# Transposes of the activated columns in groups of eight, in float32r, from tiles filled by a DMA

## Chip, cores and metric

The kernel runs on one core of one Trainium2 chip. The metric is the device time of one execution in microseconds (us). The short names of the engines are those of the profile: PE is TensorE (matmul), PEld its weight load, DVE is VectorE, ACT is ScalarE, POOL is GpSimd and SP is SyncE, which here only issues DMAs.

## The reference, cut to what matters

One decoder layer over 256 tokens of width 2048, float32 throughout. An input projection, two kinds of attention and an output projection come first; then the part with the change, a feed-forward block of width 8192:

```python
x = x + _rmsnorm(mixed @ w_out[layer], norm_attn_post[layer])

h = _rmsnorm(x, norm_mlp_pre[layer])
u = jnp.square(jax.nn.relu(h @ w_up[layer]))        # 256 x 8192
x = x + _rmsnorm(u @ w_down[layer], norm_mlp_post[layer])
```

## The kernel before, in words

**Split operands.** Every large matmul is done on float32r operands. A float32 value is split into `hi`, which ACT writes rounded to float32r, and `lo`, the remainder, which DVE writes; a product is then three matmuls, hi by hi, lo by hi and hi by lo (`three`, `mm`). Weights come in tiles of 128 x 1024 by DMAs that SP issues, into five `raw` buffers, and are split into eight pairs of `hi` and `lo` buffers, six tiles ahead of their use (`Weights`, `W_AHEAD`).

**The up phase.** The 8192 columns of `w_up` are taken in eight column groups of 1024 (`for j in range(FF // CW)`). Of each group four accumulators of 128 tokens x 512 columns are built in four banks of PSUM, for token block b = 0, 1 and column half n = 0, 1. The first group takes sixteen plain steps over the rows of the weights. Each later group takes five plain steps (`k`, 12 matmuls each) and then three steps of seven products (`w`), with single plain steps between; the seven products need four further banks for the partial sums `m`, and these are the four banks of the previous group (`free`). At the end `close` combines the partial sums into four SBUF tiles `c0` to `c3`.

**The evacuation, `up_evac`.** Each accumulator is evacuated by a chain of its own: DVE adds its `c` tile to it (not in the first group), ACT takes the Relu with the row's scale into a float32 tile `r` (two buffers), PE transposes `r` in four pieces of 128 x 128 into the same bank, now called `rt`, and ACT squares that into `uT`, where the columns lie on partitions as the down projection needs them. The transposes go through `transpose`, which takes the float32 identity `ident` and the float32 data.

**The down phase.** For g = 0 to 15, `split_u(g)` splits `uT[g]` and `down_mm` multiplies it with `w_down`. The evacuation of the last column group runs beside its first matmuls; the banks of that group are taken over for outputs at step (0, 1).

**What sets the order.** The kernel fixes the order of every engine's instructions itself, with a model clock (`Flow`). Each matmul that is written out moves the clock on (`MM`, 0.216 us for 512 columns), each transpose by `TR` = 0.109. Chains such as `up_evac` are generators: `yield t` means that the chain goes on when the clock has moved on by t. `flow.pump()`, called after every three matmuls of the up phase and after every twelve of the down phase, lets the chains that are due write their next instructions. `flow.finish(*chains)` runs chains to their end at once, whatever their delays. The delays place an instruction in the lists; they do not make the chip wait. On the chip each engine works through its own list in order and waits by semaphores.

Of the kernel before, what the change touches and what calls it, by code (L numbers as in the profile page):

```python
# [18 lines left out]
F32 = mybir.dt.float32  # L19
F32R = mybir.dt.float32r  # L20
I32 = mybir.dt.int32
BF16 = mybir.dt.bfloat16
AF = mybir.ActivationFunctionType
OP = mybir.AluOpType
PSUM = bass.MemoryType.PSUM

P = 128
D = 2048
S = 256
NB = S // P  # L30
# [15 lines left out]
CW = 1024  # L46
# [44 lines left out]
D_X0, D_X, D_SS, D_TAB = 6.0, 1.0, 3.0, (16.0, 20.0)  # L91
D_NORM, D_HT, D_SECOND = 4.5, 1.5, 4.0

D_UP, UP_STEP = 1.8, 2.2


N_SEVEN, SUMS_AHEAD = 3, 2
# [6 lines left out]
TR = 0.109  # L104
# [121 lines left out]
def layer(nc, tc, io):  # L226
    flow = Flow()

    def pool(name, side, **kw):
        return tc.alloc_tile_pool(name=name, bufs=1, side=side, **kw)  # L230

    con = pool("con", "left")
# [7 lines left out]
    def bank(i, name):  # L240
        return ps.tile([P, 512], F32, tag=f"bank{i}", bufs=1, name=name)
# [5 lines left out]
    def acc_bank(name):  # L247
        return next_bank(0, 4, name)
# [12 lines left out]
    def transpose(out, a):  # L261
        nc.tensor.transpose(out, a, ident)  # L262
        flow.spend(TR)
# [37 lines left out]
    def up_weight(j, k):  # L301
        return io["w_up"][k * P:(k + 1) * P, j * CW:(j + 1) * CW]

    late = {}
# [29 lines left out]
    for j in range(FF // CW):  # L334
        wide_u.append([])
        for what, k in [("k", k) for k in range(KD)] if j == 0 else UP_STEPS:
            if what == "k":
                ts = [weights.plan(up_weight(j, k), 1, CW, gcol[:, 8 + k:9 + k])]
            else:
                sums, fs = seven(j, k)  # L340
                weights.first[max(len(weights.specs) - SUMS_AHEAD, after)] = sums
                ts = [weights.plan(f) for f in fs]
# [66 lines left out]
    nc.gpsimd.memset(neg_half, -0.5)  # L409
    ident = con.tile([P, P], F32, name="ident")  # L410
    make_identity(nc, ident)
    warm = con.tile([P, 1], F32, name="warm")
    nc.scalar.activation(warm, neg_half, AF.Copy)
    if N_WARM:
# [15 lines left out]
    k = 0  # L430
# [136 lines left out]
    for half in range(2):  # L567
        qkv = {}
        for nm in "qkv":
            accs = [acc for _, _, acc in proj(xT, [ch_a[half, nm]], f"{nm}{half}")]  # L570
            t = pa.tile([P, NB, 512], F32, tag=nm, name=f"{nm}_{half}")
# [135 lines left out]
    rstd2 = [None] * NB  # L707
# [79 lines left out]
    for ns in ((0, 1), (2,), (3,)):  # L787
        if len(ns) == 2:
            order = [(c, t, b) for ts in (range(6), range(6, 8)) for c in range(2) for t in ts for b in range(NB)]
        else:  # L790
            order = [(0, t, b) for t, b in in_order(8, (0, APART[0] if ns == (3,) else 0))]
        for c, b, acc in proj(mixT, [ch_o[n] for n in ns], f"o{ns[0]}", order, heads_done):
            n = ns[c]
            if not late:
# [8 lines left out]
                                  in_=io["norm_attn_post"].partition_broadcast(P).rearrange("p o d -> p (o d)"))  # L803
# [10 lines left out]

    uT, dpl = {}, {}

    def up_evac(j, b, i, acc, order, more=None):

        yield UP_STEP * order
        if more is not None:  # L820
            nc.vector.tensor_tensor(out=acc, in0=acc, in1=more, op=OP.add)  # L821
            yield 1.6
        r = late["up"].tile([P, 512], F32, tag="r", bufs=2, name=f"r{j}_{b}")
        nc.scalar.activation(r, acc, AF.Relu, scale=rstd2[b])  # L824
        yield D_UP if j > 1 else 2 * D_UP
        t = bank(i, f"rt{j}_{b}")
        for k in range(4):
            transpose(t[:, k * P:(k + 1) * P], r[:, k * P:(k + 1) * P])
        if j not in uT:
            tag = {"tag": "WT"[j // 2 - 6], "bufs": 2} if j >= 12 else {}  # L830
            uT[j] = late["up"].tile([P, CW], F32, name=f"uT{j}", **tag).rearrange("p (k s) -> p k s", k=4)
        nc.scalar.activation(uT[j][:, :, b * P:(b + 1) * P], t.rearrange("p (k s) -> p k s", k=4), AF.Square)

    def split_u(g):
        if g == 0:
# [33 lines left out]
    def all_sums():  # L869
        for kp in range(N_SEVEN - 1):  # L870
            yield from left_sums(kp)
        yield 8.0
        yield from left_sums(N_SEVEN - 1)
# [14 lines left out]
        return dict(zip(PARTS, c))  # L888

    PARTS = ((0, 0), (0, 1), (1, 0), (1, 1))  # L890
    evac = []
    for j in range(FF // CW):
        at = {bn: 4 * (j % 2) + i for i, bn in enumerate(PARTS)}
        if j == 0:
            accs = {bn: acc_bank(f"acc_u0_{bn[0]}{bn[1]}") for bn in at}
            at = {bn: (turn[0] - 3 + i) % 4 for i, bn in enumerate(at)}
        else:
            accs = {bn: bank(i, f"acc_u{j}_{bn[0]}{bn[1]}") for bn, i in at.items()}
        steps = wide_u[j]
        order = in_order(len(steps), (APART[1], 0)) if j == 0 else [(t, b) for t, (w, _, _) in enumerate(steps)  # L900
                                                                    for b in range(NB if w == "k" else 1)]
        for t, b in order:
            what, k, tiles = steps[t]
            if (j, t, b) == (0, 8, 0):
                flow.finish(*res)
                late["po"].release()
                mix.release()
                late["up"] = pool("up", "right")
                flow.start(all_sums())
            if (j, t, b) == (FF // CW - 1, 4, 0):  # L910
                weights.limit -= 1
                u_next = split_u(0)
            if j == 1 and what == "w":
                flow.until(lambda: len(sums) > k)
            if what == "k":
                w = weights.get(tiles[0])
                h_done(k, b)
                for n in range(2):
                    c = slice(n * 512, (n + 1) * 512)
                    three(accs[b, n], [tok(hT[x], k, b) for x in range(2)], [w[x][:, 0, c] for x in range(2)], t == 0, t == len(steps) - 1)  # L920
                    if j == 0 and t == len(steps) - 1:
                        evac.append(flow.start(up_evac(n, b, at[b, n], accs[b, n], 2 * b + n - 0.25 * (2 * b + n))))
                    flow.pump()
                if b == NB - 1:
                    weights.free(tiles[0])
                continue

            first, last = k == 0, k == N_SEVEN - 1
            if first:
                m = {n: bank(i, f"m{n}_{j}") for n, i in zip((1, 6, 7, 5), free)}  # L930
            s1, s2, s3, s4 = sums[k]
            a11, a12, a22 = [[tok(hT[x], 2 * k + kk, bb) for x in range(2)] for kk, bb in ((0, 0), (1, 0), (1, 1))]
            prods = ((a11, 0, 0, 1), (a12, 1, 0, (0, 0)), (s4, 1, 1, (0, 1)), (s2, 2, 0, 6), (a22, 2, 1, (1, 0)),
                     (s3, 3, 1, 7), (s1, 3, 0, 5))
            for p, (a, i, half, to) in enumerate(prods):
                w = weights.get(tiles[i])
                out = m[to] if isinstance(to, int) else accs[to]
                three(out, a, [w[x][:, half * 512:half * 512 + 512] for x in range(2)],
                      isinstance(to, int) and first, isinstance(to, int) and last)
                if p == 6 or prods[p + 1][1] != i:  # L940
                    weights.free(tiles[i])
                flow.pump()
            if last:
                more = close(j, m)
        free = [at[bn] for bn in PARTS]
        if j:
            for o, (b, n) in enumerate(PARTS):
                evac.append(flow.start(up_evac(2 * j + n, b, at[b, n], accs[b, n], o + 0.1, more[b, n])))
    u_last = evac[-4:]
    up = late["up"]  # L950

    y = [[None] * 4 for _ in range(NB)]
# [63 lines left out]
    for g, c in down_order:  # L1016
        u = us[g]
        if (g, c) == (0, 1):
            flow.finish(*u_last)
            for (b, n), to in zip(((0, 2), (0, 3), (1, 2), (1, 3)), PARTS):  # L1020
                y[b][n] = bank(at[to], f"y{b}{n}")
        if g < GT - 1:
            for kk in range(4):
                for b in range(NB):
                    down_mm(u, g, kk, b, (2 * c, 2 * c + 1))
                weights.free(down[g, c, kk])
                flow.pump()
                if kk == 0 and g + 1 not in us and (c or not g):
                    us[g + 1] = split_u(g + 1)
            if (g, c) == (0, 1):  # L1030
                weights.limit += 1
            if (g, c) == (10, 1):
                flow.start(x_back())
                for n in range(4):
                    nc.sync.dma_start(out=spare(4, n), in_=io["norm_mlp_post"][:, n * 512:(n + 1) * 512]
                                      .partition_broadcast(P).rearrange("p o d -> p (o d)"))
        else:
            for b in range(NB):
                for n in (2 * c, 2 * c + 1):
                    for kk in range(4):  # L1040
                        down_mm(u, g, kk, b, (n,))
                        flow.pump()
                    if n < 3:
                        square(n, b)
                        gain(n, b)
                if c:
                    fin = flow.start(final(b))
            for kk in range(4):
                weights.free(down[g, c, kk])
# [40 lines left out]
```

## Time and profile before

| | |
|---|---|
| Median of 3 runs | 1067.53 us (1067.42 to 1067.99) |
| The profiled execution | 1067.71 us |
| Its span, first to last instruction | 1065.5 us, 13234 instructions |
| Mean granted TensorE clock | 0.998 |
| Busy share | PE 99%, PEld 82%, DVE 66%, ACT 54%, POOL 3% |
| DMA | 206.24 MB, mean 194 GB/s |
| Transposes of the activated columns (rt) | 128, from 405.0 to 725.1 us of the span |

Matmuls on PE are pipelined: the duration of one row (0.39 us for 512 columns) holds its way through the array, and the next begins 0.23 us after it. What a matmul costs PE is therefore read from the starts of a run of rows, not from one row's duration. Rows of the timeline are start, duration, engine, line, operation, output and inputs, shape, count; in brackets stands the idle time before and what ended it. Rows of a tile give the shortest, median and longest duration in ns. Rows of the windows give the stretch, its length, the busy time and count of each engine, the granted clock, the busy share of the DMA engines and GB/s. In the rows of DMA issues the last number is the time from issue to landing in us.

### The profile page before, as it was taken

What the parts mean: (1) busy time and instruction counts of PE and PEld (TensorE: products, weight loads), DVE (VectorE), ACT (ScalarE), POOL (GpSimd) and SP (SyncE); (2) the same over time, 40 slices, a digit from 0 to 9 for tenths busy, and PEclk for the clock granted to TensorE, in tenths of its full rate; (3) what the DMA queues carried; (4) which work ended last, traced back from release to release, by engine and by line L of the source; (5) the groups of instructions that cost most, each with busy time, mean ns of one, the idle gap of its engine ahead of it and who ended that gap; (6) DMA issues with size and microseconds to landing.
All of it is one profiled execution on the core that took longest, in us unless ns stands there. A gap on an engine that the chain in (4) does not pass through costs nothing.

```text
span 1065.5 us, 13234 instructions
## 1 busy us (share of the span) xinstructions
PE 1054.4 (99%) x4915; PEld 876.8 (82%) x4915; DVE 701.8 (66%) x927; ACT 574.9 (54%) x763; POOL 27.2 (3%) x52
## 2 busy tenths in 40 slices
PE   9999999999999999999999999999999999999996
PEld 6888899888888788888888888888888888888885
DVE  6486546577556678979879888884555544556444
ACT  6664436565454576566656665665444444444441
POOL 0000000000000000000000000000000000000000
PEclk9999999999999999999999999999999999999999
DMA  9885447554356395645647565475655556685532
GB/s 300 306 278 151 143 123 234 145 171 157 121 203 212 99 334 179 219 154 197 225 155 237 169 197 168 165 253 185 209 195 194 193 193 192 195 309 195 192 115 79
DMA packets 74304, 206.24 MB, mean 194 GB/s; under 512 B 6912, under 2 KB 11520, under 8 KB 73856
## 3 DMA queue, kind: packets, MB, share of 16 engines
q1 hardware_dynamic: 68912, 187.20, 53.5%
q0 software_dynamic: 4896, 17.83, 4.7%
q8 instruction: 38, 0.62, 0.3%
q10 hardware_dynamic: 432, 0.37, 0.1%
q14 instruction: 26, 0.21, 0.1%
HBM read 201.18 MB, written 4.19 MB: 193 GB/s over the span
## 4 chain that ended last, share of the span: by engine, by line
PE 96%; DVE 1%; issue 1%; DMA 1%; ACT 0%; POOL 0%; DVEq 0%; POOLq 0%; ACTq 0%
PE y L258 32%; PE acc_u L258 25%; PE acc_o L258 8%; PE m L258 5%; PE acc_k L258 4%; PE acc_v L258 4%; PE acc_q L258 4%; PE acc_ckv L258 2%; PE acc_ukv L258 2%; PE acc_cq L258 2%; PE acc_uq L258 2%; PE rt L262 1%; PE sc_b L258 1%; PE sc_a L258 0%; PE o_a L258 0%
## 5 line engine op out<-in xcount | busy, mean ns | idle before, releaser
L269 DVE TENSOR_TENSOR lo<-raw,hi 128x1024 fp32r<-128x1024 f32 (+3 forms) x253 | 292.9, 1165 | 243.1 <-ACT hi L268 242.8
L268 ACT ACTIVATE hi<-raw 128x1024 fp32r<-128x1024 f32 (+3 forms) x253 | 253.5, 1012 | 230.4 <-PE y L258 174.3
L258 PE MATMUL y<-hi,uhi 128*128 128x512 f32 x512 | 199.5, 390 | 0.0
L258 PE MATMUL y<-lo,uhi 128*128 128x512 f32 x512 | 199.2, 389 | 0.0
L258 PE MATMUL y<-hi,ulo 128*128 128x512 f32 x512 | 160.3, 389 | 0.0
L258 PE MATMUL acc_u<-hi,hT_hi 128*128 128x512 f32 x386 | 153.3, 397 | 0.0
L258 PE MATMUL acc_u<-hi,hT_lo 128*128 128x512 f32 x386 | 150.9, 391 | 0.4 <-DVE hT_lo L269 0.4
L258 PE MATMUL acc_u<-lo,hT_hi 128*128 128x512 f32 x386 | 150.6, 390 | 0.0
L273 DVE SCALAR_TENSOR_TENSOR lo<-raw,gcol,hi 128x1024 fp32r<-128x1024 f32 x86 | 107.7, 1280 | 11.5 <-ACT hi L272 11.3
L272 ACT ACTIVATE hi<-raw,gcol 128x1024 fp32r<-128x1024 f32 x86 | 98.1, 1153 | 28.5 <-PE acc_u L258 10.9
L258 PEld LDWEIGHTS y<-lo,uhi 128*128 128x128 f32 x512 | 96.1, 188 | 20.0
L258 PEld LDWEIGHTS y<-hi,ulo 128*128 128x128 f32 x512 | 96.1, 188 | 20.0
L258 PEld LDWEIGHTS y<-hi,uhi 128*128 128x128 f32 x512 | 96.1, 188 | 19.8
L258 PEld LDWEIGHTS acc_u<-hi,hT_lo 128*128 128x128 f32 x386 | 72.4, 188 | 16.1 <-DVE hT_lo L269 0.8
L258 PEld LDWEIGHTS acc_u<-hi,hT_hi 128*128 128x128 f32 x386 | 72.5, 188 | 14.5 <-DVE c L887 0.4
L258 PEld LDWEIGHTS acc_u<-lo,hT_hi 128*128 128x128 f32 x386 | 72.6, 188 | 14.2
L268 ACT ACTIVATE hi<-raw_w 128x512 fp32r<-128x512 f32 (+1 forms) x42 | 35.4, 844 | 32.2 <-PE acc_u L258 24.3
L258 PE MATMUL acc_o<-hi,mixT_hi 128*128 128x512 f32 x128 | 51.8, 405 | 0.0
L258 PE MATMUL acc_o<-hi,mixT_lo 128*128 128x512 f32 x128 | 50.2, 392 | 0.0
L258 PE MATMUL acc_o<-lo,mixT_hi 128*128 128x512 f32 x128 | 50.0, 390 | 0.0
L269 DVE TENSOR_TENSOR lo<-raw_w,hi 128x512 fp32r<-128x512 f32 (+1 forms) x42 | 39.1, 954 | 9.0 <-ACT hi L268 8.3
L824 ACT ACTIVATE r<-acc_u,rstd_pre 128x512 f32<-128x512 f32 x32 | 21.9, 687 | 26.1 <-DVE acc_u L821 22.7
(247 smaller groups left out, 1512.5 us busy)
## 6 DMA issues: line engine op xcount, KB each, us to landing
raw<-in_w_down SPq DMA_DIRECT2D x128, 512.0 KB, 4.6
raw<-in_w_up SPq DMA_DIRECT2D x86, 512.0 KB, 4.5
raw<-in_w_in SPq DMA_DIRECT2D x55, 512.0 KB, 4.9
raw_w<-in_w_up POOLq DMA_DIRECT2D x34, 512.0 KB, 4.8
raw<-in_w_out SPq DMA_DIRECT2D x32, 512.0 KB, 4.3
raw<-in_w_in SPq DMA_DIRECT2D x16, 288.0 KB, 2.8
raw<-in_w_ukv SPq DMA_DIRECT2D x8, 512.0 KB, 4.3
raw_w<-in_w_up SPq DMA_DIRECT2D x8, 512.0 KB, 4.7
```

What stands on the lines that cost most here:

```text
L258: nc.tensor.matmul(out, a, b, start=start, stop=stop)
L262: nc.tensor.transpose(out, a, ident)
L268: nc.scalar.activation(hi, src, AF.Copy)
L269: nc.vector.tensor_tensor(out=lo, in0=src, in1=hi.bitcast(F32), op=OP.subtract)
L272: nc.scalar.activation(hi, src, AF.Copy, scale=g)
L273: nc.vector.scalar_tensor_tensor(out=lo, in0=src, scalar=g, in1=hi.bitcast(F32), op0=OP.mult, op1=OP.subtract)
L824: nc.scalar.activation(r, acc, AF.Relu, scale=rstd2[b])
```

## The change

The two chains of a token block, one for each column half, become one chain `up_evac(j, b, ...)`. It writes two additions, then two Relu activations, into the `c` tiles in place. Behind each Relu ACT issues a DMA that copies the 128 x 512 float32 words into a tile `rr` declared float32r (two buffers). After D_RR = 4.6 on the model clock come eight transposes in a row, with `rr` and an identity `ident_r` both declared float32r and the output bank read as float32r; `ident_r` is filled once at the start by a DMA that ACT issues. Two Square activations follow. The chain of b = 1 starts 5.6 (D_B1) after that of b = 0. Ahead of the first product of the seven of the next column group, `flow.finish(*evac)` now writes out whatever is left of the chains.

```diff
-D_UP, UP_STEP = 1.8, 2.2
+D_RR, D_B1 = 4.6, 5.6
...
     make_identity(nc, ident)
+    ident_r = con.tile([P, P], F32R, name="ident_r")
+    nc.scalar.dma_start(out=ident_r.bitcast(F32), in_=ident)
...
-    def up_evac(j, b, i, acc, order, more=None):
-
-        yield UP_STEP * order
-        if more is not None:
-            nc.vector.tensor_tensor(out=acc, in0=acc, in1=more, op=OP.add)
-            yield 1.6
-        r = late["up"].tile([P, 512], F32, tag="r", bufs=2, name=f"r{j}_{b}")
-        nc.scalar.activation(r, acc, AF.Relu, scale=rstd2[b])
-        yield D_UP if j > 1 else 2 * D_UP
-        t = bank(i, f"rt{j}_{b}")
-        for k in range(4):
-            transpose(t[:, k * P:(k + 1) * P], r[:, k * P:(k + 1) * P])
...
-        nc.scalar.activation(uT[j][:, :, b * P:(b + 1) * P], t.rearrange("p (k s) -> p k s", k=4), AF.Square)
+    def up_evac(j, b, banks, accs, delay, more):
+
+
+        up, tiles = late["up"], []
+        yield delay
+        for n in range(2):
+            if j:
+                nc.vector.tensor_tensor(out=accs[n], in0=accs[n], in1=more[n], op=OP.add)
+                yield 0.8
+        if j:
+            yield 0.8
+        for n in range(2):
+            r = more[n] if j else up.tile([P, 512], F32, tag=f"c{2 + n}", bufs=1, name=f"r{b}{n}")
+            nc.scalar.activation(r, accs[n], AF.Relu, scale=rstd2[b])
+            rr = up.tile([P, 512], F32R, tag="rr", bufs=2, name=f"rr{j}_{b}{n}")
+            nc.scalar.dma_start(out=rr.bitcast(F32), in_=r)
+            tiles.append(rr)
+        yield D_RR
+        ts = [bank(banks[n], f"rt{j}_{b}{n}") for n in range(2)]
+        for t, rr in zip(ts, tiles):
+            for k in range(4):
+                nc.tensor.transpose(t[:, k * P:(k + 1) * P].bitcast(F32R), rr[:, k * P:(k + 1) * P], ident_r)
+                flow.spend(TR)
+        for n, t in enumerate(ts):
+            i = 2 * j + n
...
+            nc.scalar.activation(uT[i][:, :, b * P:(b + 1) * P], t.rearrange("p (k s) -> p k s", k=4), AF.Square)
+            yield 0.8
...
             if first:
+                flow.finish(*evac)
                 m = {n: bank(i, f"m{n}_{j}") for n, i in zip((1, 6, 7, 5), free)}
...
-        if j:
-            for o, (b, n) in enumerate(PARTS):
-                evac.append(flow.start(up_evac(2 * j + n, b, at[b, n], accs[b, n], o + 0.1, more[b, n])))
-    u_last = evac[-4:]
+        evac = [flow.start(up_evac(j, b, [at[b, n] for n in range(2)], [accs[b, n] for n in range(2)], 0.2 + b * D_B1,
+                                   [more[b, n] for n in range(2)] if j else None)) for b in range(NB)]
...
         if (g, c) == (0, 1):
-            flow.finish(*u_last)
+            flow.finish(*evac)
```

More of the change, by code (lines that the diff above doesn't have):

```diff
@@ L815, in layer @@
     uT, dpl = {}, {}
-    def up_evac(j, b, i, acc, order, more=None):
-        yield UP_STEP * order
-        if more is not None:
-            nc.vector.tensor_tensor(out=acc, in0=acc, in1=more, op=OP.add)
-            yield 1.6
-        r = late["up"].tile([P, 512], F32, tag="r", bufs=2, name=f"r{j}_{b}")
-        nc.scalar.activation(r, acc, AF.Relu, scale=rstd2[b])
-        yield D_UP if j > 1 else 2 * D_UP
-        t = bank(i, f"rt{j}_{b}")
-        for k in range(4):
-            transpose(t[:, k * P:(k + 1) * P], r[:, k * P:(k + 1) * P])
[L829 to L832, printed above, removed]
+    def up_evac(j, b, banks, accs, delay, more):
[21 more added lines that the diff above has]
+            i = 2 * j + n
+            if i not in uT:
+                tag = {"tag": "WT"[j - 6], "bufs": 2} if j >= 6 else {}
+                uT[i] = up.tile([P, CW], F32, name=f"uT{i}", **tag).rearrange("p (k s) -> p k s", k=4)
+            nc.scalar.activation(uT[i][:, :, b * P:(b + 1) * P], t.rearrange("p (k s) -> p k s", k=4), AF.Square)
+            yield 0.8
     def split_u(g):
@@ L890, in layer @@
     PARTS = ((0, 0), (0, 1), (1, 0), (1, 1))
-    evac = []
     for j in range(FF // CW):
@@ L920, in layer @@
                     three(accs[b, n], [tok(hT[x], k, b) for x in range(2)], [w[x][:, 0, c] for x in range(2)], t == 0, t == len(steps) - 1)
-                    if j == 0 and t == len(steps) - 1:
-                        evac.append(flow.start(up_evac(n, b, at[b, n], accs[b, n], 2 * b + n - 0.25 * (2 * b + n))))
                     flow.pump()
```

## The prediction

> **What bounds the kernel now.** First the page's busy times, then its chain that ended last, then the view of waits for TensorE.
>
> ```profile
> PE 1054.4 (99%) x4915; PEld 876.8 (82%) x4915; DVE 701.8 (66%) x927; ACT 574.9 (54%) x763; POOL 27.2 (3%) x52
> PE 96%; DVE 1%; issue 1%; DMA 1%; ACT 0%; POOL 0%; DVEq 0%; POOLq 0%; ACTq 0%
> PE warm L419 <- DVE zero L416: 1.2, 1, 1.2
> PE acc_q L258 <- ACT hi L268: 1.1, 1, 1.1
> PE acc_u L258 <- DVE hT_lo L269: 0.4, 1, 0.4
> PE qrt L262 <- DVE qT L656: 0.2, 1, 0.2
> ```
>
> TensorE (PE) is busy 99% of the span, 96% of the chain is PE, and all its recorded waits together are 2.9 us. It runs one list of matmuls in order. Whatever shortens an item of that list shortens the kernel; whatever makes PE wait once lengthens it by the whole wait.
>
> **What the transposes cost now.** The answer for the tile rt, two stretches of the timeline, and matmuls of two widths:
>
> ```profile
> L262 PE MATMUL rt<-ident,r x128: 270/272/273, 405.0 to 725.1; 128*128 128x128 f32 x128
> 405.00 0.60 PE L262 MATMUL rt<-ident,r 128*128 128x128 f32 x4
> 405.36 0.48 PE L258 MATMUL acc_u<-hi,hT_hi 128*128 128x512 f32 x1
> 405.67 0.40 PE L258 MATMUL acc_u<-lo,hT_hi 128*128 128x512 f32 x1
> 717.95 1.03 PE L262 MATMUL rt<-ident,r 128*128 128x128 f32 x8
> 441.82 0.39 PE L258 MATMUL acc_u<-lo,hT_hi 128*128 128x512 f32 x1
> 446.81 0.39 PE L258 MATMUL acc_u<-hi,hT_lo 128*128 128x512 f32 x1
> 150.09 0.29 PE L258 MATMUL acc_ckv<-lo,xT_hi 128*128 128x288 f32 x1
> 152.88 0.29 PE L258 MATMUL acc_ckv<-lo,xT_hi 128*128 128x288 f32 x1
> ```
>
> The last two pairs of rows are the first and the last of 23 and of 22 matmuls in a row: one float32r matmul of 512 columns takes 4.99/22 = 0.227 us of PE's path, one of 288 columns 2.79/21 = 0.133 us. From 405.00 to 405.67 PE did four transposes and one 512-column matmul, so four cost 0.67 - 0.23 = 0.44 us, 0.11 each. The group of eight that stands there already costs the same: (1.03 - 0.27)/7 = 0.109. So 128 transposes take 14.1 us, and grouping them in eights is worth nothing by itself.
>
> **The cheaper transpose.** No row shows a float32r transpose. The line through the two float32r widths falls 0.094 us over 224 columns; at 128 columns it gives 0.133 - 0.067 = 0.066 us. That is one end. The other is that transposes stay at 0.11, because what passes through is still a 32-bit word. I take 0.066, since the 288-column row is of the declared type; the gain is then 128 x 0.044 = 5.6 us, if PE never waits.
>
> **What has to happen between the two groups.** Each column group j is now evacuated in two halves, b = 0 and b = 1: two additions, two Relu activations, two copies by DMA from the c tiles into the rr tiles, then eight transposes, and two Square activations. The order of the built program on ScalarE (ACT) around the second half of j = 1, the same for j = 1 to 6:
>
> ```
> 355 L847 uT_4180<-rt_00    (Square, b=0, first half)
> 356 L832 c_1_4039<-acc_u_10 (Relu, b=1)
> 357 L834 DMACopy rr_10
> 358 L832 c_1_4040<-acc_u_11 (Relu, b=1)
> 359 L834 DMACopy rr_11
> 360 L847 uT_4188<-rt_01
> ```
>
> ACT works in order, so the Relu of b = 1 cannot start before the Square behind rt_00, which waits for PE's transposes rt_00. And on PE only 12 matmuls stand between rt_01 and rt_10, where `flow.finish(*evac)` puts the second group ahead of the first m product; the delay D_RR = 4.6 is cut short there. Behind rt_10 the whole list of matmuls is queued. Rows for that chain:
>
> ```profile
> 454.63 0.60 PE L262 MATMUL rt<-ident,r 128*128 128x128 f32 x4
> 455.27 0.60 ACT L832 ACTIVATE uT<-rt 128x512 f32<-128x512 f32 x1 [0.68 <-PE rt L262]
> 455.76 0.68 ACT L824 ACTIVATE r<-acc_u,rstd_pre 128x512 f32<-128x512 f32 x1
> L447 ACTq DMA_DIRECT2D gcol<-in_gains x1: 380/380/380, 25.1 to 25.1; - x1
> L262 PEld LDWEIGHTS rt<-ident,r x128: 138/140/142, 404.8 to 725.0; 128*128 128x128 f32 x128
> L258 PEld LDWEIGHTS acc_ckv<-hi,xT_hi x64: 187/187/191, 146.9 to 177.8; 128*128 128x128 f32 x64
> out<-uT SPq DMA_DIRECT2D x6, 256.0 KB, 2.5
> raw<-in_w_in SPq DMA_DIRECT2D x16, 288.0 KB, 2.8
> raw<-in_w_up SPq DMA_DIRECT2D x86, 512.0 KB, 4.5
> x<-in_x SPq DMA_DIRECT2D x8, 256.0 KB, 6.5
> 416.00:720.00 304.00, 303.99 (x1391) 251.35 (x1390) 259.97 (x291) 189.93 (x215) 17.28 (x32) 1.00 0.59 195
> ```
>
> Count from T, the start of rt_00 on PE. The Square starts 0.64 after the transposes' start now; with four shorter ones 0.64 - 3 x 0.042 = 0.51. The Relu follows 0.49 later and lasts 0.68, so it ends at T + 1.68. The DMA copy waits for it and its issue holds ACT's queue 0.38 us, as in the row of a DMA issued by ACT: T + 2.06. The second Relu ends at T + 2.74, and the second copy is issued there. It lands L later.
>
> L for 256 KB from SBUF to SBUF is in no row. Below lies 2.5 us (256 KB stored when little else moved), above 4.5 (512 KB in this very stage); 6.5 came only where eight loads stood in a burst. The DMA engines are 0.59 busy in the stage, by the windows row, and two copies overlap. I take 3.0, near the 288 KB loads (2.8), which also ran beside other traffic. Then rr_11 is there at T + 5.74; its weight load (0.14) and four transposes (0.26) end at T + 6.14.
>
> Before, the same work (12 matmuls and 16 transposes) took 12 x 0.227 + 16 x 0.11 = 4.48 us. So each of the six events j = 1 to 6 costs 6.14 - 4.48 = 1.66 us more, cheaper transposes already counted: 10.0 us. PE is through its 12 matmuls at T + 0.53 + 2.72 = 3.25, and waits the rest of the time.
>
> A page of the Trainium skill, "DMA: Bandwidth & Descriptors", section "Anatomy of one DMA", gives 2.0 us plus the bytes at 436 GB/s, an estimate of 2.6 us here, most of the fixed part being the receipt of the write. The 2.5 us of the 256 KB row agrees with it. By it each event costs 1.26 and the whole sum is 7.1 us in place of 10.0.
>
> **The other parts.**
> - j = 0: 24 matmuls stand between the groups, 5.44 us, so PE reaches rt_10 at T + 5.97, after rr_11 has landed. Gain 16 x 0.044 = 0.7 us.
> - j = 7, in the down phase: the Relu of b = 1 stands ahead of the Square, but its copy must wait until rt_00 has read the rr buffer (two buffers). Issue about T + 0.5, Relu 0.38 + 0.68 later, second copy at T + 1.56, landed at T + 4.56, end at T + 4.96; 12 matmuls between: 0.5 us more.
> - First groups (b = 0): 48 matmuls stand ahead of them, 10.9 us. Now the first addition and Relu come early:
>
> ```profile
> 493.23 0.69 DVE L821 TENSOR_TENSOR acc_u<-acc_u,c 128x512 f32<-128x512 f32 x1
> 493.96 0.69 ACT L824 ACTIVATE r<-acc_u,rstd_pre 128x512 f32<-128x512 f32 x1 [2.58 <-DVE acc_u L821]
> 495.51 0.60 PE L262 MATMUL rt<-ident,r 128*128 128x128 f32 x4
> ```
>
>   This transpose has 24 matmuls of its group ahead of it (5.44 us), so the group began at 490.07 and its Relu ran at + 3.9. After the change the second copy is issued about + 5.7 and lands at + 8.7: cover of 2.2 us, gone only if L is over 5.2. I cost it at nothing.
> - Start: ACT now waits for the identity matrix and issues its copy before its table load.
>
> ```profile
> 1.05 0.29 POOL masks.py:199 TENSOR_SCALAR_AFFINE_SELECT ident<-ident 128x128 f32<-128x128 f32 x1
> 0.74 1.28 ACT L413 ACT_TABLE_LOAD   x1 [0.74 <-PEq L1085]
> 2.92 0.51 ACT L272 ACTIVATE xT_hi<-xraw 128x256 fp32r<-128x256 f32 x1 [0.68 <-DMA xraw<-in_xt]
> 3.98 0.63 ACT L268 ACTIVATE hi<-raw 128x512 fp32r<-128x512 f32 x1 [0.55 <-DMA raw<-in_w_in]
> ```
>
>   Identity at 1.34, issue to 1.72, table to 3.0, so xT_hi at 3.2 in place of 2.92; the next activation waits for a load until 3.98 anyway. 64 KB more among the first loads: 0 to 0.4 us, I take 0.2.
> - Stalls of ACT in its copies: the splits of weights run six tiles ahead (W_AHEAD), and where a seven-product step uses a tile fastest, 21 matmuls go to four tiles, 1.2 us each: 7 us cover an ACT that stands still for 3. SP's own queue is moved past nothing; the copies add 32 x 0.26 = 8.4 MB beside it. Nothing.
>
> Sum: 10.0 + 0.5 - 0.7 + 0.2 = + 10.0 us. The profiled execution took 1067.71, the median is 1067.53, 0.2 less: **1077.5 us**.
>
> **Rivals.**
> 1. *The copies land before PE asks* (faster). Place: the DMA behind the Relu of b = 1. Nothing waits if L is at most 0.77 (T + 2.74 + L against T + 3.51); the sum falls with 7 us for each us of L, is zero at L = 1.6, and better than - 2.1 us below L = 1.3. Fully hidden: 1067.5 - 5.6 + 0.2 = 1062. For it: a copy inside SBUF might land sooner than any row here; against: the shortest row of this size is 2.5 us. Chance 0.06; between 1.3 and 1.9, no change that can be measured, 0.03.
> 2. *The change doesn't make transposes cheaper* (0.11 stays). Then the Square is at T + 0.64, the event 1.97 long, sum 11.8 + 0.8 + 0.2 = 12.8: 1080. For it: the 32-bit word passes either way, and a float32r weight load lasts 187 ns in its row, one of the transposes now 140. Chance 0.24.
> 3. *Copies as slow as the weights' loads*, L = 4.5, since they share the engines with one load nearly always under way: events 3.16, j = 7 2.0, j = 0 now 0.4 longer, so 19.0 + 2.0 + 0.4 + 0.2 = 21.6: 1089. Chance 0.15.
> 4. *PE's clock falls in the gaps.* At the start PE ran at a lower rate:
>
> ```profile
> 1.20 1.89 PE L419 MATMUL warm<-zero 128*128 128x512 bf16 x4 [1.20 <-DVE zero L416]
> 1.20 3.60 PE L419 MATMUL warm<-zero 128*128 128x512 bf16 x8 [1.20 <-DVE zero L416]
> ```
>
>   Four matmuls took 1.71 us there, 0.43 each, nearly twice 0.227. If each of six gaps brought that back for some 3.5 us, 1.7 us more each: 10 more, 1088. My gaps are about 1.5 and 0.8 us, with transposes between. The Trainium skill, "TensorE: Matmul & The Clock Gate", Part 1, puts the fall after a whole idle window of some 3.4 us; no run here shows it. Chance 0.04.
>
> The forecast, L between 2.2 and 4 with cheaper transposes, has 0.48.
>
> **How the numbers follow.** With L = 2.3 the sum is 5 us; L = 4.5 gives 21.6. The range 1072 to 1089 holds the forecast, rival 2 and most of rival 3. A measurement here can tell 0.2%, 2.1 us: faster 0.06, same 0.03, slower 0.91.
>
> **What would show it.** In the changed kernel's waits: PE's weight load of rt waiting for the DMA into rr, for rr_10 about 1.4 us and again for rr_11 about 0.7, in j = 1 to 7, some 13 us in all; PE's busy share near 98%; rt rows about 228 ns long, not 272; rr copies landing in 2.5 to 3.5 us. The forecast is wrong if rt waits for no DMA, or only in a few groups, or if b = 0 groups wait as well.

## The result, and the profile after

The changed kernel takes 1095.91 us (median of six runs, 1087.98 to 1101.13), beside 1067.76 for the kernel before on the same chip: a ratio of the means of 1.0251, with a 95% interval of 1.0202 to 1.0300. The direction was forecast; the size was not: 28 us were lost, where 10 were forecast, and 1096 lies above the range of 1072 to 1089.

The profiled execution took 1101.13 us, its span is 1099.4 at a mean clock of 0.985. First come the busy times and the chain that ended last of its page (the shares that the page gives for it add up to some 60% only), then the view of waits for PE and its weight loads (what waited, for whom, sum in us, times, longest):

```profile
PE 1066.3 (97%) x4915; PEld 883.2 (80%) x4915; DVE 702.3 (64%) x927; ACT 575.4 (52%) x763; POOL 27.1 (2%) x52
PE 54%; DMA 3%; issue 1%; ACT 1%; DVE 1%; ACTq 0%; DVEq 0%; POOLq 0%; POOL 0%
PE rt L840 <- DMA rr<-c: 17.0, 7, 3.1
PE rt L840 <- ACT uT L847: 2.7, 6, 0.5
```

The two numbers to compare are PE's idle time and its busy time. Idle is 1099.4 - 1066.3 = 33.1 us, against 11.1 before: 22.0 more. Busy is 11.9 more although each transpose became cheaper. 22.0 + 11.9 is the whole difference of the spans, 33.9. So there are two losses, and the view of waits shows only one. The 2.7 us put down to ACT are waits for the first copy: in all six the weight load of rt_10 begins 0.10 us behind the landing of that copy, just as in the waits put down to the DMA, and 0.00 to 0.10 us behind the end of the Square that is named.

The first loss is seen in the timelines of PE and ACT. These are the second groups (b = 1) of j = 1 and of j = 2; below, each such group of j = 1 to 6 is called an event:

```profile
458.78 0.81 PE L840 MATMUL rt<-ident_r,rr 128*128 128x128 f32 x8
460.48 0.47 ACTq L834 DMA_DIRECT2D rr<-c  x1
461.72 0.49 ACTq L834 DMA_DIRECT2D rr<-c  x1
462.00 0.39 PE L258 MATMUL acc_u<-hi,hT_lo 128*128 128x512 f32 x1
462.92 0.51 PE L840 MATMUL rt<-ident_r,rr 128*128 128x128 f32 x4 [0.52 <-ACT uT L847]
464.92 0.65 PE L840 MATMUL rt<-ident_r,rr 128*128 128x128 f32 x4 [1.49 <-DMA rr<-c]
465.37 0.76 PE L258 MATMUL m<-hi,hT_hi 128*128 128x512 f32 x1
...
505.66 0.81 PE L840 MATMUL rt<-ident_r,rr 128*128 128x128 f32 x8
507.37 0.47 ACTq L834 DMA_DIRECT2D rr<-c  x1
508.61 0.47 ACTq L834 DMA_DIRECT2D rr<-c  x1
508.90 0.39 PE L258 MATMUL acc_u<-hi,hT_lo 128*128 128x512 f32 x1
513.32 0.72 PE L840 MATMUL rt<-ident_r,rr 128*128 128x128 f32 x4 [3.05 <-DMA rr<-c]
513.84 0.76 PE L258 MATMUL m<-hi,hT_hi 128*128 128x512 f32 x1
```

T is the start of rt_00 on PE, as in the prediction. With T = 458.78, the second copy is issued at T + 2.94 and PE goes on at T + 6.59. With T = 505.66 the issue is at T + 2.95, all but the same, but PE goes on at T + 8.18. The copies of the two events landed 3.1 and 4.6 us after their issue; the six waits for rr_11 of j = 1 to 6 are 1.49, 3.05, 1.47, 3.08, 2.42 and 3.07 us.

The second loss is seen in the windows of j = 1, one microsecond each (stretch, length, then busy time and count of PE, PEld, DVE, ACT, POOL, then the granted clock, DMA share, GB/s):

```profile
463.00:464.00 1.00, 0.42 (x4) 0.28 (x4) 0.07 (x1) 1.00 (x2) 0.00 (x0) 1.00 1.08 283
464.00:465.00 1.00, 0.08 (x1) 0.11 (x2) 1.00 (x1) 0.38 (x1) 0.00 (x0) 1.00 0.92 348
465.00:466.00 1.00, 1.00 (x6) 0.90 (x7) 0.21 (x1) 0.39 (x1) 0.00 (x0) 0.52 0.28 111
466.00:467.00 1.00, 1.00 (x4) 0.81 (x3) 0.25 (x1) 1.00 (x3) 0.00 (x0) 0.50 0.77 139
467.00:468.00 1.00, 1.00 (x3) 0.77 (x3) 0.75 (x2) 1.00 (x2) 0.26 (x1) 0.50 0.89 356
468.00:469.00 1.00, 1.00 (x5) 0.77 (x4) 1.00 (x2) 0.61 (x1) 0.28 (x1) 0.77 0.16 57
```

Behind the gap the clock is at half for some 3.4 us (6.8 in j = 5), in which PE is "busy" all the time and gets half as much done: 1.7 us more. That is why the busy time grew. The six runs have mean clocks from 0.985 to 0.995; (0.998 - clock) x span is 3 to 14 us, some 10 in the median, and what is left of each run is 1083 to 1087. So by this estimate the waits cost some 15 to 19 us in every run, and the clock adds an amount that differs from run to run: hence the spread of 13 us.

The falls keep to a beat. By the granted clock of the windows view it falls at 465.04, 512.83, 560.61, 608.40, 656.19, 707.39 and 762.00: the distances are 14, 14, 14, 14, 15 and 16 times 3.413 us, to within 0.01. What fits is how much of one beat passes without 512-column matmuls: 2.8 us in the beat that ends at 465.04, and 2.67 in that of j = 3, which ends at 560.61. A gap of the same length can thus cost the clock or not, by where it lies on the beat.

### The profile page after: what moved, and what is told of

It is laid out like the page before. It is cut to its first block, busy times and chain, and to the rows that moved or that the text cites. A ratio compares the mean times of both kernels' runs of the same rounds, so it can differ in the third digit from the quotient of the medians.

```text
span 1099.4 us, 13334 instructions
## 1 busy us (share of the span) xinstructions
PE 1066.3 (97%) x4915; PEld 883.2 (80%) x4915; DVE 702.3 (64%) x927; ACT 575.4 (52%) x763; POOL 27.1 (2%) x52
## 4 chain that ended last, share of the span: by engine, by line
PE 54%; DMA 3%; issue 1%; ACT 1%; DVE 1%; ACTq 0%; DVEq 0%; POOLq 0%; POOL 0%
PE y L258 31%; PE acc_u L258 17%; PE m L258 5%; DMA rr<-c 3%; ACT c L832 1%; PE rt L840 1%; ACTq L834 0%; DVE uT L1006 0%; DVE c L903 0%; DVE lo L273 0%; ACT junkd L986 0%; DVEq L1088 0%; POOLq L1088 0%; POOL rstd_fin L1000 0%; DVE t_fin L999 0%
## 5 line engine op out<-in xcount | busy, mean ns | idle before, releaser
L273 DVE SCALAR_TENSOR_TENSOR lo<-raw,gcol,hi 128x1024 fp32r<-128x1024 f32 x86 | 108.3, 1281 | 23.8 <-ACT hi L272 23.6
L847 ACT ACTIVATE uT<-rt 128x512 f32<-128x512 f32 x32 | 18.8, 596 | 37.9 <-PE rt L840 33.4
```

What stands on the lines that cost most here:

```text
L273: nc.vector.scalar_tensor_tensor(out=lo, in0=src, scalar=g, in1=hi.bitcast(F32), op0=OP.mult, op1=OP.subtract)
L847: nc.scalar.activation(uT[i][:, :, b * P:(b + 1) * P], t.rearrange("p (k s) -> p k s", k=4), AF.Square)
```

## The experiments

**Theory A**, amended by the traces: PE waits for copies that ACT issues too late and that land slowly; the gaps also let the clock fall; nothing else costs anything. **Rival B**: the float32r transposes, or eight of them in a row, cost the time. **Rival C**: the clock falls for another reason than the gaps.

### rounded: no copy, the Relu writes rr itself

```diff
-            nc.scalar.activation(r, accs[n], AF.Relu, scale=rstd2[b])
             rr = up.tile([P, 512], F32R, tag="rr", bufs=2, name=f"rr{j}_{b}{n}")
-            nc.scalar.dma_start(out=rr.bitcast(F32), in_=r)
+            nc.scalar.activation(rr, accs[n], AF.Relu, scale=rstd2[b])
```

> The Relu writes the float32r tile itself and there is no copy: the words that the transposes read are rounded, so the u of the result is not the float32 one; all else, the order of the matmuls and the dtype of the transposes included, is as in the changed kernel. Theory A (the wait for the copies and the clock that falls behind it are the whole loss): no wait of rt over 0.2 us, mean clock 0.998 as before, time 1065 us (the 1067.5 of before less 128 transposes by 0.02). Rival B (the float32r transposes, or four tiles of them so close together, cost the time): 1080 us or more and a clock under 0.99 though no copy is left.

### plain8: the same with float32 tiles and float32 transposes

```diff
-            rr = up.tile([P, 512], F32R, tag="rr", bufs=2, name=f"rr{j}_{b}{n}")
+            rr = up.tile([P, 512], F32, tag="rr", bufs=2, name=f"rr{j}_{b}{n}")
...
-                nc.tensor.transpose(t[:, k * P:(k + 1) * P].bitcast(F32R), rr[:, k * P:(k + 1) * P], ident_r)
+                nc.tensor.transpose(t[:, k * P:(k + 1) * P], rr[:, k * P:(k + 1) * P], ident)
```

> Groups of eight and the new order alone: the Relu writes a float32 tile, the transposes are float32 as before, no copy. Theory A: 1067.5 us, within 1.5 of before, transposes 0.11 each; rounded is then 2 to 3 us faster than this one. If it is slower than 1070, the grouping has a cost of its own that the forecast put at nothing (rival B); if rounded and this one are alike within 1 us, the dtype gains nothing.

Measured: rounded 1066.08 us, ratio 0.9982 [0.9973, 0.9991]; plain8 1068.09, ratio 0.9999 [0.9991, 1.0008], beside 1068.06 for the kernel before. No row of the view of waits for PE names rt in either; the clocks are 0.997 and 0.998. Rival B falls: the grouping costs nothing, and float32r transposes gain. How much, the two timelines say, first rounded, then plain8:

```profile
410.04 0.81 PE L838 MATMUL rt<-ident_r,rr 128*128 128x128 f32 x8
410.68 0.46 PE L258 MATMUL acc_u<-hi,hT_hi 128*128 128x512 f32 x1
```

```profile
409.52 1.03 PE L838 MATMUL rt<-ident,rr 128*128 128x128 f32 x8
410.31 0.48 PE L258 MATMUL acc_u<-hi,hT_hi 128*128 128x512 f32 x1
```

Eight of them are followed by the next matmul after 0.64 us in place of 0.79: 0.019 us less for each, 2.4 us for 128. The medians differ by 2.0. The 5.6 us of the forecast were never there.

### f32copy: the copies stay, the transposes are float32

The edit is that of plain8 in the transposes, with the copy into a float32 tile kept.

> The copies stay, the transposes are float32. Theory A: the same waits as in the changed kernel (17 to 19 us) and the same fall of the clock: 1088 to 1104 us, transposes 0.11 each. Rival B (float32r transposes let the clock fall, or cause the loss): near 1068 to 1085, clock 0.998.

Measured: 1099.94 us (1096.14 to 1101.32), ratio 1.0291 [1.0268, 1.0314], clocks of 0.986 to 0.990. Waits of rt for the copies, 17.1 us in nine places, as in the changed kernel's 17.0. The copies alone thus cost all of the loss, whatever the dtype of the transposes; plain8 against this run is 32 us.

### fill: matmuls that nothing reads, in the gaps

```diff
+        for t, rr, fill in zip(ts, tiles, (12, 4)):
+            if b and 0 < j < 7:
+                for _ in range(fill):
+                    nc.tensor.matmul(t, hT[0][:, 0, :P], hT[0][:, 0:2, :].rearrange("p k s -> p (k s)"), start=True, stop=True)
```

> The changed kernel with 12 matmuls that nothing reads (512 wide, into the bank that the transposes then overwrite) ahead of rt_10 and 4 ahead of rt_11 in j = 1 to 6: 96 matmuls, some 22 us of TensorE work in the place of waits of 17.5 us. Theory A (the gaps let the clock fall, and that costs 3 to 14 us on top of the waits): clock 0.997 or 0.998, time 1086 to 1090 us, all runs within 2 us: no slower than the changed kernel's 1096 though TensorE has more to do. Rival C (the clock falls for another reason, the transposes or the copies): clock 0.985 to 0.995 as in the changed kernel, 1098 us or more.

Measured: 1096.36 us (1094.67 to 1099.26), clocks of 0.998, 0.994, 0.996 and 0.997. The windows over the same event:

```profile
463.00:464.00 1.00, 1.00 (x8) 0.83 (x8) 0.59 (x1) 0.00 (x0) 0.00 (x0) 1.00 0.62 250
464.00:465.00 1.00, 0.98 (x4) 0.46 (x3) 0.00 (x0) 0.60 (x1) 0.00 (x0) 1.00 0.63 121
465.00:466.00 1.00, 0.72 (x6) 0.68 (x7) 0.00 (x0) 0.15 (x1) 0.00 (x0) 1.00 0.82 291
466.00:467.00 1.00, 1.00 (x6) 0.82 (x5) 0.00 (x0) 1.00 (x3) 0.00 (x0) 1.00 0.33 131
```

The clock stays at 1.00 here and in five other stretches that hold the filled events, with the copies and the transposes in place: the gaps let it fall, rival C is out. The time expected (1086 to 1090) was wrong: I had reckoned that the 21.9 us of added matmuls (96 x 0.228) would lie wholly inside waits. PE's idle time fell by 14.8 only, from 33.1 to 18.3, since 12 matmuls ahead of rt_10 overran a wait of 0.5. So PE had 7.1 us more to go through, and yet the profiled execution, 1096.37, is 4.8 shorter than the changed kernel's: keeping the clock was worth some 12 us in this pair of executions. The gaps in the b = 0 groups and in j = 7 were not filled, which may be why three of the four runs are a little below 0.998; that was not tried.

### latefin: twice the matmuls between the groups

```diff
-                flow.finish(*evac)
-                m = {n: bank(i, f"m{n}_{j}") for n, i in zip((1, 6, 7, 5), free)}
+                flow.finish(evac[0])
+                m = {n: bank(i, f"m{n}_{j}") for n, i in zip((1, 6), free)}
...
+                if first and p == 4:
+                    flow.finish(evac[1])
+                    m.update({n: bank(i_, f"m{n}_{j}") for n, i_ in zip((7, 5), free[2:])})
```

> The changed kernel, with 24 matmuls in place of 12 between rt_01 and rt_10 in j = 1 to 6: b=1 is finished ahead of the fifth product of the block, b=0 ahead of the first as before; j=7 stays. Theory A (too few matmuls stand between the copy and its reader): PE comes to rt_10 at about T+6.4 (T the start of rt_00), to rt_11 at T+6.8, and the second copy is there at T+6.1 to T+7.6: waits of 0 to 0.8 in each event, some 3 in j=1..6, with 3 in j=7 and 1.5 in the b=0 groups 7 us in all in place of 22; without long gaps the clock stays at 0.996 or above: 1071 to 1078 us. Rival: the copies land when they land because TensorE stalls less only if the DMA is free; if the wait is one for DMA bandwidth or for ACT, it moves along with the transposes, and the time stays over 1088.

Measured: 1078.12 us (1077.74 to 1079.55), ratio 1.0100 [1.0085, 1.0115], clocks 0.996 to 0.999: 18 of the 28 us are back, by moving 12 matmuls; 1071 to 1078 was expected. What remains is again the landing: in j = 1 the second copy of this run landed 5.8 us after its issue.

```profile
464.49 0.45 PE L840 MATMUL rt<-ident_r,rr 128*128 128x128 f32 x4
467.10 0.53 PE L840 MATMUL rt<-ident_r,rr 128*128 128x128 f32 x4 [2.15 <-DMA rr<-c]
467.46 0.46 PE L258 MATMUL acc_u<-hi,hT_hi 128*128 128x512 f32 x1
```

Here PE had no 512-column matmul for 3.0 us, nearly as long as in the changed kernel's j = 1 (3.1, from 462.23 to 465.37), and the clock did not fall. The beat explains it: counted back in steps of 3.413 us from the one fall in this profile, at 1072.95 behind the last matmuls, beats end at 465.38 and 468.79, so the stretch lies across two of them and leaves at most 2.2 us without such matmuls in either.

The load beside this slow copy was issued 0.13 us behind it. The DMA view shows one more thing there: a 16 KB packet of an instruction queue (q8) begins 0.9 us behind the issue of the first copy, which took 3.9 us in place of 2.3. In j = 1 to 6 such a packet, 0.9 to 1.2 us behind the issue, stands at each first copy of b = 1 that took 3.7 us or more (one in fill, one here, two in best, one each in best2 and best3) and at no other; the changed kernel has none. That it is the cause is not shown.

### early2: one number, D_B1 = 4.9 in place of 5.6

> The changed kernel, with one number changed: the Relus and copies of b=1 stand in ACT's list ahead of the Squares of rt_00 and rt_01, and the copies are held up only by the transposes that read the two buffers; still 12 matmuls between rt_01 and rt_10. Theory A with ACT's list as a term of its own: the second copy is issued at about T+1.6, not T+3.0, and the wait of each of the seven events is 1.4 us less, 10 us in all: 1075 to 1084 us, clock 0.990 to 0.997. Rival: ACT's list is not what sets the issue (the landing beside the weight load does): time within 3 us of the changed kernel's, 1090 or more.

Measured: 1072.23 us (1071.10 to 1075.27), ratio 1.0045 [1.0031, 1.0059], clock 0.996 to 0.998: 24 of the 28 us are back, more than the expected 1075 to 1084 allowed. With it the order on ACT is Relu, copy, Relu, copy, and only then the Squares. Event j = 2:

```profile
501.14 1.16 PE L840 MATMUL rt<-ident_r,rr 128*128 128x128 f32 x8 [0.15 <-ACT c L832]
501.73 0.47 ACTq L834 DMA_DIRECT2D rr<-c  x1
502.97 0.47 ACTq L834 DMA_DIRECT2D rr<-c  x1
503.49 1.09 ACT L847 ACTIVATE uT<-rt 128x512 f32<-128x512 f32 x2 [0.55 <-ACT c L832]
504.96 0.97 PE L840 MATMUL rt<-ident_r,rr 128*128 128x128 f32 x8
```

The second copy is issued at T + 1.83, 1.1 us earlier than in the changed kernel, and it landed after 2.3 us, not 4.6. That is the part the expectation lacked: the two terms are one. In the changed kernel DVE's weight split (L273) frees a raw buffer, and SP issues the next load into it, just about when the second copy is issued. In j = 1 SP issued its load at 461.90, 0.18 behind the copy, which landed in 3.1; in j = 2 the load went at 508.59, 0.02 ahead of it, and the copy took 4.6. The same holds in all six events: the copy ahead of the load 3.0 to 3.1 (two), the load ahead by 0.02 to 0.56 us 4.0 to 4.6 (four). In early2 SP's loads came 1.1 us or more behind the second copy wherever the view shows one close behind it, and the seven second copies landed in 2.3 to 2.5.

The packets show what the order does. In the changed kernel's j = 2, first from 509.8 to 511.8, then from 511.8 to 513.3 (queue, packets, MB, share; q1 is SP's queue, q10 ACT's):

```profile
q1 hardware_dynamic: 113, 0.45, 78.8%
q10 hardware_dynamic: 3, 0.01, 0.8%
```

```profile
q10 hardware_dynamic: 141, 0.26, 44.4%
q1 hardware_dynamic: 33, 0.09, 37.0%
```

The copy's packets moved behind the load's. In j = 1 it is the other way round: 104 packets of q10 and none of q1 moved from 462.8 to 463.6. The limit does not lie exactly at the order of issue: in f32copy loads issued 0.01 to 0.07 us behind the copy went with landings of 4.6 to 4.7 us. The answers for the tile rr of both kernels, first the changed kernel, then early2, show the difference as a median over all copies, those of b = 0 beside POOL's loads among them:

```profile
L834 ACTq DMA_DIRECT2D rr<-c x28: 472/472/491, 452.7 to 757.6; - x28
DMA to landing us min/median/max: 2.3/4.6/6.4
```

```profile
DMA to landing us min/median/max: 2.2/3.1/6.5
```

All these copies are of the same 256 KB, so it is not their size that makes the landings differ.

### best: both, and the same in j = 7

The edits of latefin and early2, a delay of b = 1 longer by 2.0 ahead of its transposes, and in the down phase the first token block's matmuls ahead of rt_10.

> Both at once, and in j=7 the sixteen matmuls pairs of the first half of tokens ahead of rt_10, so that 24 matmuls stand between rt_01 and rt_10 in each of j = 1 to 7; nothing is left out. Theory A: the second copy is there at T+4.6 to T+6.2, PE comes at T+6.4: no wait of rt_10 or rt_11 over 0.2 us, 0.5 to 1.5 us left in the b=0 groups, clock 0.997 or 0.998: 1066 to 1068.5 us, beside 1068.1 for the kernel before, thus 0 to 2 us faster. Rival (the copies cost time by their traffic, or ACT's list is late for the Squares then, and TensorE waits for a bank): 1071 us or more.

Measured: 1071.18 us (1070.46 to 1074.32), ratio 1.0037 [1.0025, 1.0049]. It is better than the changed kernel by 25 us, but slower than the kernel before and than the 1066 to 1068.5 expected, and 5 us from rounded. No wait of a b = 1 group for its copy is left; what is left is mostly in front of the b = 0 groups, some 4 us by the starts of PE's rows. Their copies are issued in j = 1 to 5 1.1 to 3.8 us behind two loads of POOL, and land in 4.4 to 6.2 us, as in j = 3:

```profile
544.23 0.39 PE L258 MATMUL acc_u<-hi,hT_lo 128*128 128x512 f32 x1
545.32 1.16 PE L840 MATMUL rt<-ident_r,rr 128*128 128x128 f32 x8 [0.70 <-DMA rr<-c]
```

### best2 and best3: the b = 0 groups later

As best, with `D_RR, D_B1` = 6.3, 6.4 (best2) and 5.2, 4.9 (best3) in place of 4.6, 4.9.

> As the run best, but the b=0 groups stand six matmuls (1.4 us) later, 18 matmuls are left between rt_01 and rt_10 in j = 1 to 6, and rt_00 and rt_01 of j=7 stand twelve later. Theory A (best lost its 5 us against the run with rounded words to the b=0 copies, which land beside weight loads 5 to 6.5 us after their issue, and to nothing else): no wait of a b=0 group over 0.2 us, the second copy of b=1 lands 2.3 to 2.6 us after its issue at about T+1.8 and thus ahead of T+5: 1066 to 1068.5 us, 0 to 2 us faster than the kernel before or the same. Rival (the copies lengthen the weight loads, and the loss moves there): 1070 us or more with waits elsewhere than at rt.

> As the run best, with the b=0 groups three matmuls (0.7 us) later and nothing else moved on VectorE; on ACT one weight split of 1.14 us comes ahead of the Squares of rt_00 and rt_01. Theory A (the b=0 copies beside weight loads are what best still loses): the b=0 waits shrink by 0.7 us in each of six or seven events, 3 to 4 us in all: 1067 to 1069 us, the same as before within 0.2%. Rival (as in best2, ACT comes late to the Squares, and TensorE waits for the bank of m or y instead): 1073 us or more, with waits of m for ACT of 0.5 us or more in each event.

Measured: best2 1085.94 us, ratio 1.0174 [1.0153, 1.0195]; best3 1083.15, ratio 1.0136 [1.0114, 1.0159]. Both times lie where the rivals had them, and the waits are elsewhere than at rt. The reason that the rival of best2 gave, copies that lengthen the loads, is not shown. In best2 the second copies of j = 1 to 6, expected to land in 2.3 to 2.6 us, took 3.0 to 5.1, with one load 1.3 us ahead of them and, in j = 1 to 5, one 0.5 behind. The view of waits of best3:

```profile
PE m L258 <- ACT uT L847: 7.5, 6, 2.0
PE y L258 <- ACT uT L847: 4.4, 2, 4.0
```

No wait for a copy is left in it at all, but the banks of rt_00 and rt_01 are now wanted before ACT has squared them. Why ACT is late, its timeline shows:

```profile
456.83 0.69 ACT L832 ACTIVATE c<-acc_u,rstd_pre 128x512 f32<-128x512 f32 x1 [0.86 <-DVE acc_u L826]
459.39 0.47 ACTq L834 DMA_DIRECT2D rr<-c  x1
459.91 0.69 ACT L832 ACTIVATE c<-acc_u,rstd_pre 128x512 f32<-128x512 f32 x1 [2.39 <-PE rt L840]
460.62 0.47 ACTq L834 DMA_DIRECT2D rr<-c  x1
461.14 1.15 ACT L272 ACTIVATE hi<-raw,gcol 128x1024 fp32r<-128x1024 f32 x1 [0.55 <-ACT c L832]
462.20 1.06 ACT L847 ACTIVATE uT<-rt 128x512 f32<-128x512 f32 x2
```

The copy of b = 1 stands in ACT's list and waits for rt_00 to read the buffer (rt began at 458.84), and everything behind it, the weight split and the Squares, waits too. Three matmuls fewer ahead of m (9, not 12) then no longer cover it. The clock fell again with these waits (0.992 to 0.994 in best3). So in this layout the b = 0 groups wait if they come early, and m waits if they come late; with four rr buffers in place of two the copy would not have to wait for rt_00, but that was not tried.

No version with the unrounded copies beats the kernel before. The one that does, rounded, by 0.18%, has no DMA and reads rounded words.

## Why the prediction was wrong

Two terms of the sum failed: L, the landing of the second copy, was put at 3.0 us and measured 4.0 in the mean, and the clock was put at nothing and cost 3 to 14 us, some 10 in the median.

- **The place and the mechanism of the waits: right.** PE waits for rr_10 and rr_11 behind 12 matmuls, in j = 1 to 7, because the Relu and the copy of b = 1 stand behind the Square of rt_00 in ACT's list (early2 moves exactly that, and most of the loss goes).
- **L was mis-sized, and this is the step that failed first.** It was put at 3.0 in all events; it is 3.0 to 3.1 in two and 4.0 to 4.6 in four, 4.0 in the mean: 6 x 1.0 = 6 us more. The forecast took the mean busy share of the stage, 0.59, and "two copies overlap" as reasons for one value. It did not ask which load is issued in that very microsecond. Rival 3 had nearly this value, 4.5, and a chance of 0.15.
- **ACT's issue, 0.38, was 0.47:** the second copy goes at T + 2.94, not T + 2.74, 1.2 us over six events. The 0.38 row was a copy of another shape.
- **j = 7:** 0.5 was forecast; rr_10 and rr_11 landed after 5.6 and 5.0 us there, and PE waited 2.4. **b = 0**, costed at nothing with "gone only if L is over 5.2": its copies of j = 1 to 7 land in 3.5 to 6.4 us, and the groups of j = 3, 5 and 7 lost some 0.5 us each. That was the listed sign that the forecast is wrong.
- **The cheaper transpose** was 0.066 on a line through widths of 288 and 512; it is 0.11 - 0.02 = 0.09, between the two ends: 2.4 us gained of 5.6. Rival 2, no gain, is refuted by rounded against plain8.
- **The clock, rival 4, was given 0.04 and came true,** 3 to 14 us. Its reason against, "gaps of about 1.5 and 0.8 us, with transposes between", took the two gaps one by one. Together they take most of one beat: the stretch without a 512-column matmul was 3.1 us in j = 1, 4.7 in j = 2 and 2.7 in j = 3 (each from 0.23 behind the start of the last matmul to the start of the next). The forecast's own chain had such a stretch, from T + 3.25 to T + 6.14, 2.9 us. The Trainium skill, "TensorE: Matmul & The Clock Gate", Part 4, says that a transpose does not count as busy for the clock in the same way; no run here decides that, since the four transposes take only some 0.3 us of these stretches. Part 1 has the gate look at a free-running window of about 3.4 us; the trace agrees, with falls a whole number of 3.413 us apart. The whole idle window of the prediction's rival 4 was not needed: 2.67 us of 3.41 were enough in j = 3.
- **The sum.** From T to the first m product the six events took 45.5 us in the profiled execution, where 6 x 6.14 = 36.8 were forecast. Of the 8.6 us more, about 6 are L and 1.2 the issue. With some 2 us of j = 7 and 1.5 of b = 0 that makes the waits 20 to 22, in place of 10 (these terms overlap a little); the profiled execution lost 19 without the clock, the others 15 to 19. The clock took the median to 28. Rivals 3 and 4 were priced as alternatives, but one run can have both, and their prices add. The clock did not need the slow landing: in j = 1 and 3 the copy landed in 3.0 to 3.1, as forecast, and the clock fell behind the gap all the same. The range ended at rival 3 alone.

## What to carry to other kernels

Before a DMA is put between two engines, look not at the mean load of the queues but at which transfer is issued in the same microsecond: here 0.2 us of order went with 3.1 or 4.6 us. A gap on TensorE has two prices, the wait and the half clock behind it; add up the gaps that lie within 3.4 us of each other, and where they come to more than 2 us, price the clock with them. In an engine that works in order, where a copy stands in the list matters as much as when it could start: one delay on a model clock, 4.9 in place of 5.6, gave back 24 of 28 us.

## What the runs showed of the hardware

- A copy of 256 KB within SBUF lands 2.2 to 2.6 us after its issue when no load is issued near it, 2.6 to 3.3 with a 512 KB load 0.2 to 0.5 us behind it, 4.6 to 4.7 with one up to 0.07 us behind it, and mostly 3.5 to 6.7 with loads ahead of it by up to some 3.5 us. The exceptions, 3.7 to 5.8 us, stand beside a 16 KB packet of an instruction queue or behind a copy that does. The issue holds ACT for 0.47 us.
- A float32r transpose of 128 x 128 takes 0.02 us less of PE than a float32 one, though it moves the same 32-bit words.
- The clock of TensorE falls to 0.5 on a beat of 3.413 us, and for one or two beats. Over all eleven profiles, from 380 to 800 us, it fell behind every beat at full clock with 2.27 us or more without matmuls other than transposes and behind none with 2.25 or less (an estimate: each such matmul counted as 0.227 us). With the transposes counted as work the falls separate as well, near 2.0 us, so whether they count stays open.
